# A hybrid decoder trunk: two levels of the gated recurrence per set of small products, with 48 carried query columns

## The chip, the cores and the metric

The kernel runs on one core of a Trainium2 chip. Its time is the device time of one execution in microseconds (us); several executions are taken and their median is compared. A profile is one further execution, recorded by the hardware profiler: its span is the time from the first to the last instruction.

In the text TensorE is PE, its weight loads PEld, VectorE DVE, ScalarE ACT, GpSimd POOL, and SyncE, whose queue issues most DMAs, SP.

## The reference, cut to what matters

Two layers run on 256 tokens of width 1024. Each layer normalises its input, projects it to ten groups of 512 columns, mixes the tokens in three branches (block attention, a gated recurrence named HGRN2, attention to a memory of 256 tokens), gates the result, projects it back and adds it to the input. The change is in the recurrence, which for 4 heads of width 128 computes

```python
qf = jax.nn.silu(q.astype(jnp.float32))
kf = (1.0 - lb) * jax.nn.sigmoid(-fl)
...
diff = A[:, :, :, None, :] - A[:, :, None, :, :]
decay = jnp.exp(jnp.where(causal[:, :, None], diff, -jnp.inf))
scores = jnp.einsum('bhtd,bhtsd,bhsd->bhts', qc, decay, kc)
o = (jnp.einsum('bhts,bhsv->bhtv', scores, vc)
     + jnp.einsum('bhtd,bhdv->bhtv', qc * jnp.exp(A), state))
```

`A` is the running sum of the log of the forget gate. The score of query t with an earlier key s is therefore a sum over 128 channels of q times k times the product of all gates from s+1 to t, a product that differs from channel to channel.

## The kernel before, in words

**The large products.** Weights come from DRAM in 120 chunks of 128x1024 float32 on the SP queue. ACT rounds each chunk to a high part `wh` (L192, or L195 with a gain), DVE subtracts to get the low part `wl` (L204 or L207), and PE multiplies in three products (high by high, high by low, low by high), all recorded at L250. `wr` has four buffers, `wh` and `wl` three each, so a chunk's parts are made while PE works on the one or two chunks ahead of it. The groups of a layer come in the order: memory keys and values, forget gate and query of the recurrence, keys of block attention, input of the recurrence (`ih`), queries of block attention, gate, memory queries, values, two more gates, output projection. A group's results stand in `acc` banks of PSUM, of which there are four; a bank comes free when ACT and DVE have read it.

**The side work.** Everything else is written as Python generators (`g_f`, `g_q`, `g_hgrn`, `g_qk`, ...). The main loop calls `slot()` between pieces of the large products, and each `slot` moves every active generator on to its next `yield`. A scheduler then orders the instructions of each engine; products made through `mm_row` (L254) and some others are kept in program order.

**The recurrence (`g_hgrn`, L773).** Q, K and the gate F lie with channels on partitions and 4 heads x 256 tokens along the free axis. Scores are built by levels. At a level of width m, tokens are taken in pairs of sub-blocks of m; queries of the later one are multiplied by the gates from its start, keys of the earlier one by the gates to its end, and a plain product then gives the scores between the two. `carry` (L783) moves Q and K one level up (DVE, L790 and L791; into a second copy, with ACT copying the unchanged halves, L793 and L794) and multiplies neighbouring gates to the next level's gates T (L797). `diagonal` computes 32 products of 32 keys with 32 query columns each, over 128 channels, for the eight 128-token pieces (4 heads, 2 halves); each lands in one of four 32-partition strips of a PSUM tile `sd`. Two levels go into one tile: a level from `base`, the next from `other`, so 64 products. `keep` (L807) copies those scores to `hSd` that a mask `mk` selects. There are three such blocks of 64 products per layer (levels 0 and 1; 2 and 4; 8 and 16), then a fourth with 16 products of 32 columns and 16 of 64 columns for the widths 32 and 64. The rest of the program calls the blocks the first to the fourth.

**Beside it.** `g_qk` (L902) normalises and rotates q and k of block attention: squares on ACT (L603), sums on DVE (L604), a power on POOL (L915), the rotation on DVE (L918 to L925). The rotary tables `rtA` and `rtB` are made once by `g_setup`: a chain of tiny DVE operations on `rt` (L514 to L542), one Sin on ACT (L543), then POOL (L554 to L558). `g_ih` copies the recurrence's input out of its two banks (ACT, L717).

Of the kernel before, what the change touches and what calls it, by code (L numbers as in the profile page):

```python
# [12 lines left out]
F32 = mybir.dt.float32  # L13
# [32 lines left out]
def hymba_kernel(ctx: ExitStack, tc: tile.TileContext, x, mem, mem_t, positions, w_in, w_out, w_mem_kv,  # L46
# [435 lines left out]
    mk = cst.tile([128, 6, 32], U8, name="mk")  # L482
# [8 lines left out]
    def g_setup():  # L491
# [75 lines left out]
        sp = small("sp", 1)  # L567
        nc.vector.tensor_scalar(sp.bitcast(I32), si, 31, None, op0=OP.bitwise_and)
        ti = sb.tile([128, 32], I32, name="ti", tag="sg", bufs=2)
        nc.gpsimd.iota(ti, pattern=[[1, 32]], base=0, channel_multiplier=0)  # L570
        xi = sb.tile([128, 32], I32, name="xi", tag="sg", bufs=2)
        xf = sb.tile([128, 32], F32, name="xf", tag="sq", bufs=2)
        ge = sb.tile([128, 32], F32, name="ge", tag="sq", bufs=2)
        nc.vector.tensor_tensor(xi, ti, sp.bitcast(I32).to_broadcast([128, 32]), op=OP.bitwise_xor)
        nc.gpsimd.tensor_copy(xf, xi)
        nc.vector.tensor_tensor(xi, ti, sp.bitcast(I32).to_broadcast([128, 32]), op=OP.subtract)
        nc.gpsimd.tensor_copy(ge, xi)
        yield
        nc.gpsimd.tensor_scalar(ge, ge, 0.0, None, op0=OP.is_ge)
        nc.gpsimd.tensor_scalar(xf, xf, 1.0, None, op0=OP.add)  # L580
        nc.gpsimd.tensor_tensor(xf, xf, ge, op=OP.mult)
        for j, m in enumerate((0, 1, 2, 4, 8, 16)):
            nc.gpsimd.tensor_scalar(mk[:, j], xf, float(m + 1), None, op0=OP.is_ge)
# [7 lines left out]
    for tag, n, bufs in (("PTh", 1536, 1), ("PTl", 1536, 1), ("hX", 512, 1), ("qk", 1024, 1), ("sq", 512, 2),  # L591
                         ("vmh", 1024, 1), ("vml", 1024, 1), ("kmh", 1024, 1), ("kml", 1024, 1), ("as", 512, 2),
                         ("al", 256, 2), ("hF", 1024, 1), ("sg", 512, 2), ("ih", 1024, 1),
                         *((f"y{c}{br}", 1024, 1) for br in (H_, A_, M_) for c in "hl"), ("hT1", 512, 1), ("blk", 1536, 1)):
        for _ in range(bufs):
            sb.tile([128, n], F32, name="place", tag=tag, bufs=bufs)
# [105 lines left out]

    def g_q(l, h0, acc):
# [6 lines left out]
        nc.vector.tensor_tensor(T["Q"][:, cs], acc, sg, op=OP.mult)  # L710
# [62 lines left out]
    def g_hgrn(l):  # L773
# [3 lines left out]
        yield from take("PTh", "PTl")  # L777
        Qb = sb.tile([128, 1024], F32, name="hQb", tag="PTh", bufs=1)
        Kb = sb.tile([128, 1024], F32, name="hKb", tag="PTl", bufs=1)
        yield  # L780
# [25 lines left out]
        def keep(g, o, j):  # L806
            nc.vector.copy_predicated(hSd, mk[:, j][:, None, :].to_broadcast([128, 8, 32]),  # L807
                                      g[:, o:o + 256].rearrange("p (a s) -> p a s", s=32))

        nc.vector.tensor_tensor(Qb, Q, F, op=OP.mult)
# [3 lines left out]
        diagonal(g, 0, Q, K)  # L818
        diagonal(g, 256, Qb, K)
        yield 2  # L820
        Tm = carry(1, F, (Qb, K))
        keep(g, 0, 0)
        keep(g, 256, 1)
        rel()
        base, other = (Qb, K), (Q, Kb)
        for m in (2, 8, 32):
            yield
            T2 = carry(m, Tm, base, other)
            yield 2
            yield from room("sd")  # L830
            g = side_tile()
            if m < 32:
                diagonal(g, 0, *base)
                diagonal(g, 256, *other)
            else:
                for a in range(0, 8, 2):
                    for q in (0, 64):
                        for b in range(2):
                            c = (a + b) * 128 + q
                            mm_row(g[q + b * 32:q + b * 32 + 32, a * 16:a * 16 + 32],  # L840
                                   base[1][:, c:c + 32], base[0][:, c + 32:c + 64])
                for a in range(0, 8, 2):
                    for b in range(2):
                        for q in (0, 32):
                            c = (a + b) * 128
                            mm_row(g[b * 64 + q:b * 64 + q + 32, 128 + a * 32:128 + a * 32 + 64],
                                   other[1][:, c + q:c + q + 32], other[0][:, c + 64:c + 128])
            yield 2
            Tm = carry(2 * m, T2, other)
            if m < 32:  # L850
                keep(g, 0, m.bit_length())
                keep(g, 256, m.bit_length() + 1)
                rel()
                base, other = other, base
# [435 lines left out]
```

## Time and profile before

| quantity | value |
|---|---|
| median of 3 runs | 396.36 us (395.73 to 396.39) |
| the profiled execution's own time | 395.6 us |
| its span | 393.8 us |
| PE busy | 388.7 us, 99% of the span |
| DVE busy | 314.8 us, 80% |
| ACT busy | 250.9 us, 64% |
| POOL busy | 70.3 us, 18% |
| granted PE clock | 1.0 |

How to read it: PE is busy nearly all the time, but matmuls are pipelined and their ends are modelled, so a share of busy time does not say how fast PE goes. That is read from the starts of instructions in the timeline and from the waits. A product in full float32 stands in the timeline as two records, so a `diagonal` of 32 products shows as 64. In a timeline row the columns are start, duration, engine, line, operation, output and inputs, shape, count and, in brackets, the idle time before it and what ended it.

### The profile page before, as it was taken

Reading aid. Unit: us, or ns where it says so; the run is one execution under the profiler, and the core shown is the slowest. Engines: PE = TensorE matmul, PEld = TensorE weight load, DVE = VectorE, ACT = ScalarE, POOL = GpSimd, SP = SyncE. Lnnn points to the kernel's source line nnn. Section 1 sums busy time; section 2 is a strip of 40 time slices with the busy share of each in tenths; the row PEclk is TensorE's granted clock in tenths of the full one; section 3 lists DMA queues with packets and bytes.
Section 4 is the critical chain, followed back from the end, with each engine's and each line's share of the span. In section 5 each row is a group of like instructions: output and inputs, shape, how many; then the busy total and the mean of one; then the engine's idle time right before and its main releaser. Section 6 shows DMA issues by size and latency. Waiting matters only on the chain.

```text
span 393.8 us, 7606 instructions
## 1 busy us (share of the span) xinstructions
PE 388.7 (99%) x2871; PEld 325.4 (83%) x2871; DVE 314.8 (80%) x606; ACT 250.9 (64%) x422; POOL 70.3 (18%) x109
## 2 busy tenths in 40 slices
PE   8999999999999999999999999999999999999996
PEld 6888888878788889888888888888888888888885
DVE  4789999889759997964576789799866799897643
ACT  5998746548768759653376665455865894894430
POOL 2013400604202522000000040041150063200000
PEclk9999999999999999999999999999999999999999
DMA  8986674377534989536565658745954189981612
GB/s 280 413 288 222 240 236 156 111 253 227 179 100 169 280 240 327 189 129 207 177 187 173 195 181 229 256 151 158 275 174 155 53 269 272 344 226 67 212 55 107
DMA packets 24900, 80.33 MB, mean 204 GB/s; under 512 B 3232, under 2 KB 5664, under 8 KB 24864
## 3 DMA queue, kind: packets, MB, share of 16 engines
q1 hardware_dynamic: 22304, 71.31, 55.3%
q0 software_dynamic: 2272, 8.39, 7.6%
q8 instruction: 22, 0.36, 0.4%
q10 hardware_dynamic: 288, 0.15, 0.1%
q14 instruction: 14, 0.11, 0.1%
HBM read 72.51 MB, written 7.34 MB: 203 GB/s over the span
## 4 chain that ended last, share of the span: by engine, by line
PE 91%; DVE 4%; POOL 1%; issue 1%; DMA 1%; ACT 1%; ACTq 0%; DVEq 0%
PE acc L250 63%; PE acc L1176 17%; PE sd L250 6%; PE sd L254 4%; DVE wl L204 1%; PE sd L1140 1%; PE sd L463 1%; DMA gT<-in_gains_dram 1%; ACT wh L192 1%; POOL rka L915 1%; PE sd L950 0%; PE sd L1080 0%; POOL rtB L558 0%; DVE hSd L807 0%; DVE hQb L790 0%
## 5 line engine op out<-in xcount | busy, mean ns | idle before, releaser
L204 DVE TENSOR_TENSOR wl<-wr,wh 128x1024 fp32r<-128x1024 f32 x96 | 116.9, 1218 | 40.4 <-ACT wh L192 40.2
L192 ACT CAST wh<-wr 128x1024 fp32r<-128x1024 f32 x96 | 100.8, 1050 | 69.2 <-PE acc L250 42.4
L250 PE MATMUL acc<-wh,hT 128*128 128x512 f32 x384 | 124.8, 396 | 0.0
L250 PEld LDWEIGHTS acc<-wh,hT 128*128 128x128 f32 x384 | 71.8, 188 | 16.1 <-issue 0.7
L250 PE MATMUL acc<-wl,hT 128*128 128x512 f32 x192 | 75.1, 391 | 0.0
L250 PE MATMUL acc<-hT,wh 128*128 128x512 f32 x256 | 65.2, 393 | 0.0
L250 PEld LDWEIGHTS acc<-hT,wh 128*128 128x128 f32 x256 | 45.8, 189 | 8.2 <-ACT kn L617 0.4
L250 PEld LDWEIGHTS acc<-wl,hT 128*128 128x128 f32 x192 | 36.1, 188 | 7.0
L207 DVE SCALAR_TENSOR_TENSOR wl<-wr,gT,wh 128x1024 fp32r<-128x1024 f32 (+1 forms) x29 | 31.2, 1096 | 10.5 <-ACT wh L195 10.3
L195 ACT ACTIVATE wh<-wr,gT 128x1024 fp32r<-128x1024 f32 (+1 forms) x29 | 28.7, 1005 | 14.4 <-PE acc L1176 6.5
L250 PEld LDWEIGHTS acc<-hT,wl 128*128 128x128 f32 x256 | 35.2, 190 | 2.5
L1176 PE MATMUL acc<-wl,yh 128*128 128x512 f32 (+1 forms) x96 | 37.2, 387 | 0.0
L1176 PE MATMUL acc<-wh,yl 128*128 128x512 f32 (+1 forms) x96 | 36.8, 387 | 0.0
L250 PE MATMUL acc<-hT,wl 128*128 128x256 f32 x256 | 36.6, 284 | 0.0
L1176 PE MATMUL acc<-wh,yh 128*128 128x512 f32 (+1 forms) x96 | 30.3, 390 | 0.0
L250 PE MATMUL acc<-wh,mTh 128*128 128x512 f32 x64 | 25.4, 400 | 0.2 <-DVE mTh L402 0.2
L250 PE MATMUL acc<-wh,mTl 128*128 128x512 f32 x64 | 24.8, 390 | 0.0
L1001 ACT ACTIVATE P<-P,nba,rq 128x128 f32<-128x128 f32 (+1 forms) x32 | 17.1, 535 | 8.3 <-DVE nba L995 8.3
L1176 PEld LDWEIGHTS acc<-wh,yh 128*128 128x128 f32 x96 | 18.0, 188 | 3.9 <-issue 0.3
L1176 PEld LDWEIGHTS acc<-wh,yl 128*128 128x128 f32 x96 | 18.0, 188 | 3.7
L1176 PEld LDWEIGHTS acc<-wl,yh 128*128 128x128 f32 x96 | 18.1, 188 | 3.5
L250 PE MATMUL acc<-wl,mTh 128*128 128x512 f32 x64 | 20.2, 392 | 0.0
(222 smaller groups left out, 575.0 us busy)
## 6 DMA issues: line engine op xcount, KB each, us to landing
wr<-in_w_in_dram SPq DMA_DIRECT2D x80, 512.0 KB, 4.3
wr<-in_w_out_dram SPq DMA_DIRECT2D x24, 512.0 KB, 4.4
wr<-in_w_mem_kv_dram SPq DMA_DIRECT2D x15, 512.0 KB, 4.4
there<-blk POOLq DMA_DIRECT2D x4, 768.0 KB, 5.4
PT<-there POOLq DMA_DIRECT2D x16, 192.0 KB, 6.0
there<-blk SPq DMA_DIRECT2D x4, 512.0 KB, 3.7
xs<-in_x_dram SPq DMA_DIRECT2D x2, 512.0 KB, 8.6
memr<-in_mem_dram SPq DMA_DIRECT2D x2, 512.0 KB, 6.7
```

The source lines that it names most:

```text
L192: nc.scalar.copy(whs[i], raws[i])
L195: nc.scalar.activation(whs[i][:, sl], raws[i][:, sl], AF.Copy, scale=gT[:, g:g + 1])
L204: nc.vector.tensor_tensor(wls[i], raws[i], whs[i].bitcast(F32), op=OP.subtract)
L207: ins = nc.vector.scalar_tensor_tensor(wls[i][:, sl], in0=raws[i][:, sl], scalar=gT[:, g:g + 1], in1=whs[i][:, sl].bitcast(F32), op0=OP.mu ...
L250: nc.tensor.matmul(o, lhsT=a, rhs=b, start=s, stop=e)
L254: tc.keep_in_program_order(nc.tensor.matmul(o, lhsT=a, rhs=b, start=s, stop=e))
L463: ins = nc.tensor.transpose(pt[:, j * 256 + t * 128:j * 256 + (t + 1) * 128], xn[t][:, k * 128:(k + 1) * 128], ident)
L915: nc.gpsimd.tensor_tensor(r[:, t8], ms[:, t8], pw[:, :8], op=OP.pow)
L1001: nc.scalar.activation(P[:, i, kc[t]], P[:, i, kc[t]], AF.Exp, bias=nb[:, c:c + 1], scale=rq[:, r:r + 1], accum_out=sm[:, c:c + 1])
L1140: nc.tensor.transpose(pt[:, i * 256 + t * 128:i * 256 + (t + 1) * 128], P[:, t, i, b * 128:(b + 1) * 128], ident)
L1176: ins = nc.tensor.matmul(a, lhsT=y, rhs=wt[:, cs], start=n == (0 if to is None else nk - 2) and j == 0, stop=n == nk - 1 and j == 2)
```

## The change

The three blocks of 64 products of 32 columns become three blocks of 32 products of 48 columns. Keys are no longer carried for the second level of a block: both levels of a block use the same 32 key columns, and the queries are laid out several times instead. In the first block each pair of tokens has three query columns: both queries as they are, and the later one carried over one token. In the second (m = 2) and the third (m = 8), each four sub-blocks of m tokens have six sub-blocks of query columns: the second, third and fourth as they stand at their own start, the third and fourth carried back over one more sub-block, the fourth carried over two. The fill and the carries of the queries move to new operations; `g_q` writes Q twice with a stride of three (now in the buffer PTh); there are eight masks in place of six and eight `keep` operations in place of six, on fewer columns each. The fourth block and all behind it stay as they were.

The core of the diff, without the set-up of the masks:

```diff
-            T["Q"] = sb.tile([128, 1024], F32, name="hQ", tag="hq0", bufs=1)
+            yield from take("PTh", "PTl")
+            T["Q"] = sb.tile([128, 512, 3], F32, name="hQ1", tag="PTh", bufs=1)
...
-        nc.vector.tensor_tensor(T["Q"][:, cs], acc, sg, op=OP.mult)
+        nc.vector.tensor_tensor(T["Q"][:, h0 * 128:h0 * 128 + 256, 0:2], pairs(acc, 2), pairs(sg, 2), op=OP.mult)
...
-        def diagonal(g, o, q, k):
+        def row(q, m):
+            g = side_tile()
             for i in range(8):
                 for j in range(4):
-                    c = slice(i * 128 + j * 32, i * 128 + j * 32 + 32)
-                    mm_row(g[j * 32:j * 32 + 32, o + i * 32:o + i * 32 + 32], k[:, c], q[:, c])
+                    c = i * 4 + j
+                    mm_row(g[j * 32:j * 32 + 32, i * 48:i * 48 + 48].rearrange("p (n m) -> p n m", m=m),
+                           K[:, c * 32:c * 32 + 32], q(c))
...
-        nc.vector.tensor_tensor(Qb, Q, F, op=OP.mult)
+        nc.vector.tensor_tensor(Q[:, :, 2], Q[:, :, 1], F2[:, :, 1], op=OP.mult)
         yield 2
         yield from room("sd")
-        g = side_tile()
-        diagonal(g, 0, Q, K)
-        diagonal(g, 256, Qb, K)
+        g = row(lambda c: Q[:, c * 16:c * 16 + 16], 3)
+        Tm = sb.tile([128, 512], F32, name="hT1", tag="hT1", bufs=1)
+        nc.vector.tensor_tensor(Tm, F2[:, :, 0], F2[:, :, 1], op=OP.mult)
         yield 2
-        Tm = carry(1, F, (Qb, K))
-        keep(g, 0, 0)
-        keep(g, 256, 1)
-        rel()
-        base, other = (Qb, K), (Q, Kb)
-        for m in (2, 8, 32):
...
+        n4 = sb.tile([128, 128, 7, 2], F32, name="hQ2", tag="PTl", bufs=1)
+        nc.vector.tensor_tensor(n4[:, :, 0:4], Q[:, :, 0:3:2].rearrange("p (g a) i -> p g a i", a=4),
+                                F2[:, :, 0].rearrange("p (g a) -> p g a", a=4)[:, :, :, None]
+                                .to_broadcast([128, 128, 4, 2]), op=OP.mult)
+        nc.vector.tensor_tensor(K2[:, :, 0], K2[:, :, 0], F2[:, :, 1], op=OP.mult)
+        keep(g[:, :, :, 0:2], 0, 2, 0, 2)
+        keep(g[:, :, :, 2:3], 1, 2, 1, 2)
+        rel()
+        for m in (2, 8):
...
+            nc.vector.tensor_tensor(q[:, :, 4:6], q[:, :, 2:4], by(1, 2), op=OP.mult)
+            nc.vector.tensor_tensor(q[:, :, 6:7], q[:, :, 5:6], by(1, 1), op=OP.mult)
+            yield 2
+            yield from room("sd")
+            b = 8 // m
+            g = row(lambda c: q[:, c * b:c * b + b, 1:7].rearrange("p g a i -> p g (a i)") if b > 1
+                    else q[:, c, 1:7].rearrange("p a i -> p (a i)")[:, None, :], 6 * m)
+            nc.vector.tensor_tensor(T4[:, :, 2], T4[:, :, 2], T4[:, :, 3], op=OP.mult)
+            nc.vector.tensor_tensor(T4[:, :, 1], T4[:, :, 1], T4[:, :, 2], op=OP.mult)
+            Tn = sb.tile([128, n], F32, name=f"hT{m}", tag=f"hT{m}", bufs=1)
+            nc.vector.tensor_tensor(Tn, T4[:, :, 0], T4[:, :, 1], op=OP.mult)
+            yield 2
...
+            nc.scalar.copy(to(0, 1), split(q[:, :, 0:1]))
+            nc.vector.tensor_tensor(to(1, 1), split(q[:, :, 1:2]), split(by(0, 1)), op=OP.mult)
+            nc.vector.tensor_tensor(to(2, 2), split(q[:, :, 4:7:2]), split(by(0, 1, 2)), op=OP.mult)
+            nc.vector.tensor_tensor(K4[:, :, 0:3], K4[:, :, 0:3], by(1, 3), op=OP.mult)
+            for k, (lo, hi, at) in enumerate(((1, 4, 0), (2, 4, 3), (3, 4, 5))):
+                keep(g[:, :, :, at * m:(at + hi - lo) * m], (2 if m == 2 else 5) + k, 4 * m, lo * m, hi * m)
+            rel()
+            Tm = Tn
+        base = n4, K
+        other = [sb.tile([128, 1024], F32, name=n, tag=t, bufs=1) for n, t in (("hQb", "PTl"), ("hKb", "PTh"))]
```

The scheduler also orders the neighbourhood anew; lines below the change carry higher numbers in the changed kernel. Three places of layer 0 matter to what follows.

PE around the third block, before. The names `acc_1164` and `acc_1165` are the two banks (tokens 0 to 127 and 128 to 255) of the group that follows, the queries of block attention:

```order
L250 MATMUL acc_927<-wh_903,hT_160 128x512
L254 MATMUL sd_1096<-hQ_712,hKb_792 32x32 x32
L254 MATMUL sd_1096<-hQb_791,hK_591 32x32 x32
L250 MATMUL acc_1164<-wh_949,hT_160 128x512
L250 MATMUL acc_1164<-wl_1044,hT_160 128x512
L250 MATMUL acc_1164<-wh_949,hT_160 128x512
L250 MATMUL acc_1165<-wh_949,hT_160 128x512
```

and in the changed kernel, where the same two banks are named `acc_1070` and `acc_1071`:

```order
L254 MATMUL sd_1018<-hQ3_982,hK_592 32x48 x32
L250 MATMUL acc_1070<-wh_913,hT_160 128x512
L250 MATMUL acc_1070<-wl_980,hT_160 128x512
L250 MATMUL acc_1070<-wh_913,hT_160 128x512 x2
L250 MATMUL acc_1070<-wl_980,hT_160 128x512
L250 MATMUL acc_1070<-wh_913,hT_160 128x512
L250 MATMUL acc_1070<-wh_978,hT_160 128x512
L250 MATMUL acc_1070<-wl_1009,hT_160 128x512
L250 MATMUL acc_1070<-wh_978,hT_160 128x512 x2
L250 MATMUL acc_1070<-wl_1009,hT_160 128x512
L250 MATMUL acc_1070<-wh_978,hT_160 128x512
L250 MATMUL acc_1070<-wh_1007,hT_160 128x512
```

The two products by 32 columns became one by 48, and the group behind them now does twelve products of its first bank before it touches its second. Its banks are other ones than before: in the placement of the built program they were those of the block-attention keys, and are now those that `ih` is copied out of.

ACT around the Sin of the rotary tables (`sc_164`), before:

```order
L603 ACTIVATE sq<-acc 128x512
L543 ACT_TABLE_LOAD
L543 ACTIVATE sc_164<-rt 128x32
L192 CAST wh<-wr 128x1024
L793 COPY hQb<-hQ 128x64x8
L192 CAST wh<-wr 128x1024
L794 COPY hK<-hKb 128x64x8
L192 CAST wh<-wr 128x1024
L717 COPY ih<-acc 128x512
L192 CAST wh<-wr 128x1024
L717 COPY ih<-acc 128x512
```

and in the changed kernel:

```order
L599 ACTIVATE sq<-acc 128x512
L863 COPY hQ<-hQ_982 128x32x8
L192 CAST wh<-wr 128x1024 x2
L789 COPY hQb<-hQ 128x16x32
L192 CAST wh<-wr 128x1024
L543 ACT_TABLE_LOAD
L543 ACTIVATE sc_164<-rt 128x32
L717 COPY ih<-acc 128x512
L192 CAST wh<-wr 128x1024
L717 COPY ih<-acc 128x512
L790 COPY hKb<-hK 128x16x32
```

The Sin moved behind three casts and the copy of the fourth block's queries, and stands directly ahead of the first copy of `ih`.

DVE ahead of the `wl` of the first chunk of that group (chunk 24 of 120), before; `tm` is a piece of the rotation of the keys, and waits for `rtB`:

```order
L790 TENSOR_TENSOR hQ<-hQ,hT_938 128x128x4
L920 TENSOR_TENSOR tm<-acc,rtB 128x8x8
L922 TENSOR_TENSOR tm<-acc,rtB 128x8x8
L920 TENSOR_TENSOR tm<-acc,rtB 128x8x8
L922 TENSOR_TENSOR tm<-acc,rtB 128x8x8
L791 TENSOR_TENSOR hKb<-hKb,hT_938 128x128x4
L807 COPY_PREDICATED hSd<-mk,sd 128x256
L790 TENSOR_TENSOR hQb<-hQ,hT_1054 128x64x8
L925 TENSOR_TENSOR kr<-kr,tm 128x8x16 x2
L791 TENSOR_TENSOR hK<-hKb,hT_1054 128x64x8
L807 COPY_PREDICATED hSd<-mk,sd 128x256
L204 TENSOR_TENSOR wl<-wr,wh 128x1024
```

and in the changed kernel, from the `wl` of chunk 23 to that of chunk 24:

```order
L204 TENSOR_TENSOR wl<-wr,wh 128x1024
L951 TENSOR_SCALAR msa<-ssa 128x8
L866 TENSOR_TENSOR hK<-hK,hT_844 128x128x6
L808 COPY_PREDICATED hSd<-mk,sd 128x32x6
L865 TENSOR_TENSOR hQ<-hQ_982,hT_952 128x32x16
L843 TENSOR_TENSOR hT_952<-hT_952 128x32
L541 TENSOR_SCALAR rt<-rt 128x16
L204 TENSOR_TENSOR wl<-wr,wh 128x1024
```

The rotation of the keys no longer stands between the two `wl`; it moved behind the `wl` of chunk 26.

More of the change, by code (lines that the diff above doesn't have):

```diff
@@ L565, in g_setup @@
         nc.gpsimd.memset(hSd, 0.0)
[L567 to L577, printed above, removed]
-        yield
[L579 to L583, printed above, removed]
+        d = sb.tile([128, 3, 32], I32, name="ti", tag="sg", bufs=2)
+        for q, w in enumerate((1, 2, 8)):
+            nc.gpsimd.iota(d[:, q], pattern=[[1, 32 // w], [0, w]], base=0, channel_multiplier=0)
+        sp = small("sp", 3)
+        xf = sb.tile([128, 3, 32], F32, name="xf", tag="sq", bufs=2)
+        for q, w in enumerate((0, 1, 3)):
+            j = sp[:, q:q + 1].bitcast(I32)
+            nc.vector.tensor_scalar(j, si, 31, w, op0=OP.bitwise_and, op1=OP.logical_shift_right)
+            nc.vector.tensor_tensor(d[:, q], d[:, q], j.to_broadcast([128, 32]), op=OP.subtract)
+        nc.gpsimd.tensor_copy(xf, d)
+        yield
+        for j, (q, least) in enumerate(((0, 0), (0, 1), (1, 1), (1, 2), (1, 3), (2, 1), (2, 2), (2, 3))):
+            nc.gpsimd.tensor_scalar(mk[:, j], xf[:, q], float(least), None, op0=OP.is_ge)
     setup = g_setup()
@@ L776, in g_hgrn @@
         St = hST.rearrange("p h t s -> p (h t) s")
[L777 to L780, printed above, removed]
         def halves(a, m):
@@ L814, in g_hgrn, with keep, part @@
-        nc.vector.tensor_tensor(Qb, Q, F, op=OP.mult)
+                    c = i * 4 + j
+                    mm_row(g[j * 32:j * 32 + 32, i * 48:i * 48 + 48].rearrange("p (n m) -> p n m", m=m),
+                           K[:, c * 32:c * 32 + 32], q(c))
+            return g[:, :384].rearrange("p (a n m) -> p a n m", a=8, m=m)
+        def keep(g, j, n, lo, hi):
+            def part(a):
+                return a.rearrange("p a (n m) -> p a n m", m=n)[:, :, :, lo:hi]
+            nc.vector.copy_predicated(part(hSd), part(mk[:, j][:, None, :].to_broadcast([128, 8, 32])), g)
@@ L815, in g_hgrn @@
+        base = n4, K
+        other = [sb.tile([128, 1024], F32, name=n, tag=t, bufs=1) for n, t in (("hQb", "PTl"), ("hKb", "PTh"))]
+        yield
+        T2 = carry(32, Tm, base, other)
         yield 2
@@ L817, in g_hgrn @@
         g = side_tile()
-        diagonal(g, 0, Q, K)
-        diagonal(g, 256, Qb, K)
-        yield 2
-        Tm = carry(1, F, (Qb, K))
-        keep(g, 0, 0)
-        keep(g, 256, 1)
-        rel()
-        base, other = (Qb, K), (Q, Kb)
-        for m in (2, 8, 32):
[L827 to L830, printed above, removed]
-            g = side_tile()
[L832 to L854, printed above, removed]
+        for a in range(0, 8, 2):
+            for q in (0, 64):
+                for b in range(2):
+                    c = (a + b) * 128 + q
+                    mm_row(g[q + b * 32:q + b * 32 + 32, a * 16:a * 16 + 32],
+                           base[1][:, c:c + 32], base[0][:, c + 32:c + 64])
+        for a in range(0, 8, 2):
+            for b in range(2):
+                for q in (0, 32):
+                    c = (a + b) * 128
+                    mm_row(g[b * 64 + q:b * 64 + q + 32, 128 + a * 32:128 + a * 32 + 64],
+                           other[1][:, c + q:c + q + 32], other[0][:, c + 64:c + 128])
+        yield 2
+        carry(64, T2, other)
         S2 = St.rearrange("p (a b) s -> p a b s", b=2)
```

31 lines of the change are left out of this document (26 added, 5 removed).

## The prediction

> **What bounds the kernel now.** I read the page, then who PE waits for, then the chain of work that ended last. From the page, the span and the busy time of each engine:
>
> ```profile
> span 393.8 us, 7606 instructions
> ## 1 busy us (share of the span) xinstructions
> PE 388.7 (99%) x2871; PEld 325.4 (83%) x2871; DVE 314.8 (80%) x606; ACT 250.9 (64%) x422; POOL 70.3 (18%) x109
> ```
>
> All waits of PE, longest first (us in total, times, longest):
>
> ```profile
> PE sd L250 <- DVE dm L378: 1.0, 1, 1.0
> PE sd L254 <- ACT wh L192: 0.2, 1, 0.2
> PE acc L250 <- DVE mTh L402: 0.2, 1, 0.2
> ```
>
> PE waits 1.4 us in all, 1.2 of it at the start. The kernel is bound by PE's own work: a product left out shortens it by what that product takes on PE, unless a new wait eats the gain. The chain (start, us, what) runs over PE in layer 1 and shows the four blocks, L254, among large products. Its counts mix loads and records, so only its times are used:
>
> ```profile
> 85.59 0.65 PE sd L254 x32
> ...
> 106.02 1.96 PE sd L254 x24
> ...
> 252.42 1.23 PE sd L254 x82
> ...
> 260.69 1.30 PE sd L254 x98
> ...
> 269.01 1.30 PE sd L254 x98
> ...
> 277.33 0.88 PE sd L254 x63
> ```
>
> The three blocks of 1.23, 1.30 and 1.30 us are what the change cuts; layer 0 has the same three. In layer 0 the chain comes onto PE only at 85.59, in the fourth block. (106.02 is the first use of the attention keys `kT`.)
>
> **PE, the main term.** The timeline of PE in layer 1 (start, us, and at the end the count of records), second and fourth block:
>
> ```profile
> 260.62 0.76 PE L254 MATMUL sd<-hQb,hK 128*32 128x32 f32 x64
> 261.23 0.75 PE L254 MATMUL sd<-hQ,hKb 128*32 128x32 f32 x64
> 261.92 0.50 PE L250 MATMUL acc<-wh,hT 128*128 128x512 f32 x1
> ...
> 277.26 0.46 PE L254 MATMUL sd<-hQb,hK 128*32 128x32 f32 x32
> 277.54 0.68 PE L254 MATMUL sd<-hQ,hKb 128*32 128x64 f32 x32
> 278.14 0.50 PE L250 MATMUL acc<-wh,hT 128*128 128x512 f32 x1
> ```
>
> Starts are what counts. From 260.62 to 261.23, 64 records of 32 columns take 0.61 us, 9.5 ns each; the next 64 take 0.69 to the first large product, so 0.08 is the change back. With 64 columns, 32 records take 0.60 - 0.08 = 0.52 us, 16.3 ns each. The trace has no record of 48 columns. It lies between these two, and I take the middle, 12.9 ns, since the price already grows with the columns. A block then has 64 records of 12.9 ns and the change, 0.83 + 0.08 = 0.91 us, against 1.23, 1.30 and 1.30: 3.83 - 2.73 = 1.1 us a layer, 2.2 us for both. At the price of 32 columns a block takes 0.69 and both layers give 3.5 us; at the price of 64 it takes 1.12 and they give 0.9. The number of changes between small and large products stays as it is.
>
> Here the Trainium skill has a rule: "TensorEngine Tiling (Array Packing)", section Instruction Overhead, says that each matmul has about 60 cycles of overhead, so that fewer columns than that cost the same. By it 48 columns cost what 32 do, and the two layers would give 3.5 us. The rows show a price that grows from 32 to 64, 9.5 to 16.3 ns, which speaks against it; it is a rival below.
>
> **The waits in layer 0.** PE's timeline at the first large products behind the third block, and in the fourth block:
>
> ```profile
> 77.84 0.50 PE L250 MATMUL acc<-wh,hT 128*128 128x512 f32 x1
> 78.18 0.48 PE L250 MATMUL acc<-wl,hT 128*128 128x512 f32 x1
> ...
> 84.95 0.46 PE L254 MATMUL sd<-hQb,hK 128*32 128x32 f32 x32
> 85.59 0.65 PE L254 MATMUL sd<-hQ,hKb 128*32 128x64 f32 x32 [0.17 <-ACT wh L192]
> ```
>
> and DVE's around them:
>
> ```profile
> 61.16 1.22 DVE L204 TENSOR_TENSOR wl<-wr,wh 128x1024 fp32r<-128x1024 f32 x1 [0.27 <-ACT wh L192]
> 62.30 0.26 DVE L521 SCALAR_TENSOR_TENSOR rt<-rt 128x16 f32<-128x16 f32 x2
> ...
> 73.48 0.23 DVE L920 TENSOR_TENSOR tm<-acc,rtB 128x64 f32<-128x64 f32 x1 [1.75 <-POOL rtB L557]
> ...
> 76.90 1.20 DVE L204 TENSOR_TENSOR wl<-wr,wh 128x1024 fp32r<-128x1024 f32 x1
> ...
> 84.76 0.68 DVE L791 TENSOR_TENSOR hKb<-hK,hT 128x512 f32<-128x512 f32 x1
> ```
>
> The 32 records that took 0.28 us in layer 1 (277.26 to 277.54) take 0.64 here, so 0.36 us are a wait. The profile names ACT's cast, but the 64-column products read DVE's carried keys, and L791 ends at 85.44, just ahead. And the `wl` of chunk 24 ends at 78.10 and is read at 78.18: DVE is 0.08 us ahead. DVE's order here decides whether the gain stays.
>
> **DVE and ACT.** Durations by form, from the groups of instructions (us in all, mean ns of one):
>
> ```profile
> L755 DVE TENSOR_TENSOR ys<-sd,zT 128x512 f32<-128x512 f32 x8 | 5.4, 680 | 0.0
> ...
> L807 DVE COPY_PREDICATED hSd<-mk,sd 128x256 f32<-128x256 uint8 x12 | 5.3, 443 | 0.0
> ...
> L814 DVE TENSOR_TENSOR hQb<-hQ,hF 128x1024 f32<-128x1024 f32 x2 | 2.5, 1226 | 0.0
> ...
> L790 DVE TENSOR_TENSOR hQb<-hQb,hF 128x512 f32<-128x512 f32 x2 | 1.4, 684 | 0.0
> ...
> L797 DVE TENSOR_TENSOR hT<-hT 128x256 f32<-128x256 f32 x2 | 0.8, 420 | 0.0
> ```
>
> This L790 reads and writes every second element and takes 684 ns, the plain L755 680, so I price strided and broadcast forms by their elements alone, 1.06 ns each beyond 512 ((1226 - 684) / 512): 768 elements 0.95 us, 128 some 0.28. Before, DVE does 14 carries of 0.68, L814 with 1.23, and 2.0 for the gates T: 12.8 us a layer. Now it does eleven operations of 512 (Q's third column, T, K, two more at each of two levels, four for the widths 32 and 64), 7.5; the tile of 1024, 1.23; four of 256, 1.7; two of 768, 1.9; smaller ones for T, 1.6: 13.9 us, 1.1 more. The eight `keep` cover 1152 columns where six covered 1536, about 2.6 us either way by 443. ACT loses four copies a layer and gains two of half the size. In layer 1 all this lies beside the large products. Layer 0 is walked through by the changed order, each operation starting its duration less 0.08 behind the last, as 62.30 follows 61.16. ACT's rows for it:
>
> ```profile
> 66.39 1.28 ACT L543 ACT_TABLE_LOAD   x1
> 67.68 0.23 ACT L543 ACTIVATE sc<-rt 128x32 f32<-128x32 f32 x1
> ...
> 76.27 0.57 ACT L717 COPY ih<-acc 128x512 f32<-128x512 f32 x1
> ```
>
> The queries of levels 2 and 4 are made ahead of the `wl` of chunk 21, which slips from 61.16 to about 61.4 and takes 1.1. From there to the end of L865 at the second level stand two `wl`, six operations of 512, three of 256, two of 128, one of 768, three `keep` and small ones, 10.0 us: L865 ends near 72.6, and the `wl` of chunk 24 near 73.9. PE reads it at 78.18 less the 1.1 it has gained, 77.1: DVE is 3.2 us ahead instead of 0.08, because the rotation of the keys has left this path. Behind it come the fourth block's queries, two `wl`, then `tm`, which waits for POOL. The Sin starts near 75.5 (below) and not at 67.68. POOL's steps from there to the first `rtB` took until 73.48, 5.8 us, with 2.1 of L915 between that now go first: `tm` starts near 79.2, the keys' carry ends near 81.9, and the fourth block, wanted at 84.95 - 1.1 = 83.9, waits no more: 0.36 us gained. The `wl` of chunk 27 ends near 84.5, two us ahead of its use. The keys' transpose then sends `kT` 4 to 5 us later on SP, past one more load; its first use at 106.02 leaves that covered. The masks come from POOL long before their use.
>
> **The sum.** 2.2 + 0.36 = 2.6 us. The profiled execution, 395.6 us with 1.8 outside its span, would come to 393.0. It lies 0.8 under the median of the runs, so from 396.36 I forecast 393.8 us.
>
> **The rivals.** *48 columns at the price of 32.* 3.5 + 0.36 leave 392.5 us. For it: the four strips work at once, and what else bounds 9.5 ns is not shown. Against it: the growth to 16.3. The page's rule of 60 cycles says the same.
>
> *Part of the gain is lost.* 48 columns at the price of 64 give 0.9 + 0.36, 395.1 us; a new wait of 1.3 us on PE gives the same.
>
> *PE waits for the banks of `ih`, and it is slower.* The queries of block attention now use the banks that L717 empties, behind the Sin. Behind L865 at 72.6 follow the copy L789 (0.6), a cast (1.0), the table load (1.3), the Sin and the first L717 (0.7): the bank is free near 76.2. PE wants it at 77.84 - 1.1 = 76.7, so 0.5 us are left. Each further us on this path stalls PE by one; from 3.1 nothing is gained, from 3.9 it is slower. The new strided forms ahead of L865 hold 5376 elements; if they cost twice as much, 5.7 us, PE waits 5.2 and the time is 399.0 us. Against: 684 beside 680. The Trainium skill, "ScalarE: Activation LUTs", section What ACT_TABLE_LOAD costs, adds a drain of about 1.38 us to every table load; an estimate from it is a wait of 0.9 here, 394.7 us. The trace disagrees: the Sin starts 1.29 us after its load began.
>
> *Nothing comes of it.* At half more for the strided forms PE waits 2.3 us, and 396.1 us is no difference.
>
> **How the numbers follow.** Chances: forecast 0.54, price of 32 columns 0.14, part lost 0.19, nothing 0.08, slower 0.05. About 0.2%, 0.8 us, is what a measurement can tell here, so under 395.6 is faster. The first two cases and three quarters of the third are: 0.82. Within 0.2% is the rest of the third and the fourth, 0.13; slower 0.05. The price of 48 columns alone runs from 392.5 to 395.1; the range, 392.4 to 395.7, takes this in, and leaves out the last two cases and a little of the third.
>
> **What would show it.** Right: L254 has 64 records a block, starting near 12.9 ns apart; blocks near 0.9 us in the chain; the `wl` of chunk 24 some 3 us ahead of its use; no wait of PE at the fourth block of layer 0 nor behind the third. Wrong: the first large product behind the third block starts late with ACT's L717 as what it waited for; L835 or L865 takes well over 0.7 us; blocks still take 1.2.

## The result and the profile after

| quantity | before | after |
|---|---|---|
| median of 6 runs | 395.85 us (395.73 to 396.39) | 392.64 us (392.32 to 393.37) |
| the profiled execution's own time | 395.6 us | 392.6 us |
| its span | 393.8 us | 390.8 us |

The ratio is 0.9918, 95% interval 0.9908 to 0.9928: 3.2 us less. The forecast was 2.6 us less, 393.8 us, and 0.5 of the 1.16 us between it and 392.64 is that it started from a median of three runs, 396.36, where six gave 395.85. The other 0.6 is gain that the forecast did not have.

The page of the changed kernel, span and busy times:

```profile
span 390.8 us, 6833 instructions
## 1 busy us (share of the span) xinstructions
PE 385.8 (99%) x2487; PEld 322.9 (83%) x2487; DVE 316.2 (81%) x621; ACT 248.0 (63%) x418; POOL 73.4 (19%) x109
```

All its waits of PE (us in total, times, longest):

```profile
PE sd L250 <- DVE dm L378: 1.0, 1, 1.0
PE acc L250 <- ACT mTh L404: 0.3, 1, 0.3
```

Both are at the start. The wait in layer 0's fourth block is gone and none has taken its place. The chain that ended last, the blocks of small products (start, us):

```profile
60.59 0.82 PE sd L254 x64
67.75 0.82 PE sd L254 x64
75.82 0.82 PE sd L254 x64
84.11 0.88 PE sd L254 x63
...
251.20 0.82 PE sd L254 x64
```

Blocks of 1.23, 1.30 and 1.30 us have become 0.82 each, in both layers: 1.37 us a layer. The chain now runs over PE in layer 0 too. PE's timeline in the fourth block of layer 0:

```profile
84.04 0.46 PE L254 MATMUL sd<-hQ,hK 128*32 128x32 f32 x32
84.31 0.68 PE L254 MATMUL sd<-hQb,hKb 128*32 128x64 f32 x32
```

From start to start the 32 records take 0.27 us here, 0.64 before.

**A ruler that the start does not bend.** PE's first us differ by up to 2.7 us between the traces: its waits for the first chunks differ, and in two traces (rot24 and late1) the granted clock is 0.5 for 3.4 us near the start. So the kernels below are also compared by the starts of large products (outputs named `acc`), of which every trace has 1568: from the 61st to the last; from the 241st to the 601st, which holds layer 0's blocks; from the 1001st to the 1301st, which holds layer 1's. Stretches without blocks agree: before and after, from the 601st to the 1001st both take 92.45 us.

| kernel | median, us | 61st to last | layer 0 | layer 1 |
|---|---|---|---|---|
| before | 395.85 | 369.79 | 95.37 | 82.51 |
| after | 392.64 | 366.64 | 93.55 | 81.18 |
| cols64 | 394.15 | 367.84 | 94.18 | 81.73 |
| cols32 | 392.9 | 366.64 | 93.55 | 81.17 |
| two24 | 396.95 | 370.45 | 95.74 | 82.80 |
| rot24 | 396.82 | 370.25 | 95.92 | 82.41 |
| strips | 402.28 | 376.20 | 98.36 | 85.94 |
| parts | 425.39 | 400.32 | 110.12 | 98.25 |
| later3 | 395.95 | 369.43 | 95.05 | 82.52 |
| late1 | 394.54 | 368.08 | 94.98 | 81.18 |
| layer1 | 395.72 | 369.31 | 96.36 | 81.08 |
| dve2 | 393.12 | 366.66 | 93.54 | 81.21 |
| mg12 | 392.98 | 366.43 | 93.16 | 81.33 |
| mgx | 392.68 | 365.91 | 93.16 | 80.81 |

Experiments ran on chips on which the kernel before took 396.15 to 396.46 us, so their medians stand 0.3 to 0.6 us high beside the first two rows. parts was executed four times, and two of them ran at a lower granted clock and longer (430.87 and 432.31 us), so its row has the median of the two others.

By the ruler the change gains 3.15 us: 1.82 in layer 0 and 1.33 in layer 1. Layer 0 has the same 1.37 of the blocks and the 0.36 of the wait; under 0.1 us is left over. The scheduler orders every kernel anew: later3 has PE's order of before, but for the block that was moved, and late1 that of the changed kernel until after the fourth block; in most of the others some block stands a few large products elsewhere, and it is said where that matters.

### The profile page after: what moved, and what is told of

It is laid out like the page before. It is cut to its first block, busy times and chain, and to the rows that moved or that the text cites. A ratio compares the mean times of both kernels' runs of the same rounds, so it can differ in the third digit from the quotient of the medians.

```text
span 390.8 us, 6833 instructions
## 1 busy us (share of the span) xinstructions
PE 385.8 (99%) x2487; PEld 322.9 (83%) x2487; DVE 316.2 (81%) x621; ACT 248.0 (63%) x418; POOL 73.4 (19%) x109
## 4 chain that ended last, share of the span: by engine, by line
PE 98%; DMA 1%; DVE 0%; ACT 0%; issue 0%; DVEq 0%
PE acc L250 69%; PE acc L1213 17%; PE sd L250 6%; PE sd L254 4%; PE sd L1177 1%; PE sd L463 1%; DMA gT<-in_gains_dram 1%; PE sd L987 0%; PE sd L1117 0%; ACT wh L195 0%; DVE xs L1247 0%; DVE xs L1254 0%; ACT mTh L404 0%; DVEq L1254 0%
## 5 line engine op out<-in xcount | busy, mean ns | idle before, releaser
L250 PE MATMUL acc<-wh,hT 128*128 128x512 f32 x384 | 122.9, 394 | 0.0
L195 ACT ACTIVATE wh<-wr,gT 128x1024 fp32r<-128x1024 f32 (+1 forms) x29 | 28.7, 1006 | 14.3 <-PE acc L1213 6.5
L1038 ACT ACTIVATE P<-P,nba,rq 128x128 f32<-128x128 f32 (+1 forms) x32 | 17.1, 536 | 8.3 <-DVE nba L1032 8.3
L952 POOL TENSOR_TENSOR rka<-msa,pw 128x8 f32<-128x8 f32 x4 | 9.9, 2475 | 58.2 <-DVE msa L951 58.2
```

The lines of the kernel that those rows point to most:

```text
L195: nc.scalar.activation(whs[i][:, sl], raws[i][:, sl], AF.Copy, scale=gT[:, g:g + 1])
L250: nc.tensor.matmul(o, lhsT=a, rhs=b, start=s, stop=e)
L952: nc.gpsimd.tensor_tensor(r[:, t8], ms[:, t8], pw[:, :8], op=OP.pow)
L1038: nc.scalar.activation(P[:, i, kc[t]], P[:, i, kc[t]], AF.Exp, bias=nb[:, c:c + 1], scale=rq[:, r:r + 1], accum_out=sm[:, c:c + 1])
```

## The experiments

Theory A is that of the prediction, in the sizes that the trace of the changed kernel shows: PE bounds, a small product's price grows with its columns, and DVE's order in layer 0 decides whether the gain stays.

### What a product of 48 columns costs: cols64 and cols32

```diff
-                    mm_row(g[j * 32:j * 32 + 32, i * 48:i * 48 + 48].rearrange("p (n m) -> p n m", m=m),
-                           K[:, c * 32:c * 32 + 32], q(c))
+                    w = 64 if c < 31 else s
+                    mm_row(g[j * 32:j * 32 + 32, i * 64:i * 64 + w], K[:, c * 32:c * 32 + 32],
+                           q[:, c * s:c * s + w])
```

> The changed kernel with its 48 query columns widened to 64 (31 of 32 products of a block; the 16 more are computed and not used). Theory A, a record's price grows with its columns: in the changed kernel's trace four records of 48 columns, one for each strip, take 42.5 ns and four of 64 columns in the fourth block 55.8, 10.6 and 14.0 ns a record. A block grows by 62 x 3.4 ns = 0.21 us, from 0.82 to 1.03; six blocks give 1.3 us, 393.9 us. Theory B, a product has a price of its own and columns do not count up to 64: blocks stay at 0.82 and the time at 392.6 us.

The first block in the chain, and the others are like it:

```profile
60.97 1.02 PE sd L254 x62
```

0.20 more a block; six are 1.2, and the ruler has 367.84 - 366.64 = 1.20. Theory A holds.

```diff
-                    mm_row(g[j * 32:j * 32 + 32, i * 48:i * 48 + 48].rearrange("p (n m) -> p n m", m=m),
+                    mm_row(g[j * 32:j * 32 + 32, i * 32:i * 32 + 32], K[:, c * 32:c * 32 + 32], q(c))
```

> The changed kernel with 32 of the 48 query columns in every product of the three blocks; a third of the scores is left out, DVE's work stays as it is. Theory A, the price grows with the columns: 8.0 ns a record as in the fourth block, 64 x 2.6 ns = 0.17 us less a block, 1.0 us in all, 391.6 us. Theory B, a price a product whatever its columns: 392.6 us, no change.

In the chain the first block of layer 1 and what the fourth became; then two of PE's waits:

```profile
251.33 0.69 PE sd L254 x50
...
273.19 0.39 PE sd L254 x32
276.52 0.58 PE sd L254 x32
```

```profile
PE acc L250 <- ACT ih L717: 0.3, 1, 0.3
PE acc L250 <- ACT wh L195: 0.2, 1, 0.2
```

The blocks came out near theory A, 0.13 less each where it had 0.17, and yet nothing is gained. In layer 0 the 0.39 us of three blocks meet a wait of 0.3 us that the changed kernel does not have, for the copy L717: the bank of `ih`. (The wait for L195 is at the start.) In layer 1 the scheduler split the fourth block in two (0.39 and 0.58 beside 0.88), and one more change between small and large products took the gain. The first is the prediction's third rival, at work here with PE less than 0.4 us earlier.

### Whether few columns stay cheap: two24, parts, rot24, strips

Each product as two of 24 columns, one behind the other in the same strip:

```diff
-                    mm_row(g[j * 32:j * 32 + 32, i * 48:i * 48 + 48].rearrange("p (n m) -> p n m", m=m),
-                           K[:, c * 32:c * 32 + 32], q(c))
+                    for u in range(2):
+                        o = i * 48 + u * 24
+                        mm_row(g[j * 32:j * 32 + 32, o:o + 24].rearrange("p (n m) -> p n m", m=min(m, 24)),
+                               K[:, c * 32:c * 32 + 32], q(c, u))
```

> The changed kernel with every product of 48 columns made as two of 24, twice the records and the same columns. Theory A, a straight line through 8.0 ns at 32 and 10.6 at 48 columns: 24 columns 6.7 ns, 128 records 0.86 us against 0.68, 0.18 more a block, 1.1 us in all, 393.7 us. Theory B, a record does not get cheaper than the 8.0 ns that 32 columns take: 128 x 8.0 = 1.02 us, 0.34 more a block, 2.1 us in all, 394.7 us. Theory C, columns alone count: no change, 392.6 us.

The first block of layer 1 in the chain, like the other two there:

```profile
254.42 1.38 PE sd L254 x102
```

1.38 us a block, over all three expectations. The kernel parts does the same in three pieces of 16 columns and four of 12.

```diff
-                    mm_row(g[j * 32:j * 32 + 32, i * 48:i * 48 + 48].rearrange("p (n m) -> p n m", m=m),
-                           K[:, c * 32:c * 32 + 32], q(c))
+                    z = 48 // parts
+                    for u in range(parts):
+                        o = i * 48 + u * z
+                        mm_row(g[j * 32:j * 32 + 32, o:o + z], K[:, c * 32:c * 32 + 32], q(c, u))
```

> The changed kernel with each product of the first and third block made as three of 16 columns, and of the second as four of 12. Theory A, the straight line: 5.4 ns a record at 16 columns, 4.8 at 12; the blocks take 192 x 5.4 + 0.14 = 1.18, 256 x 4.8 + 0.14 = 1.37 and 1.18 us against 0.82, 1.3 us more a layer, 2.5 in all, 395.2 us. Theory B, a floor at the 8.0 ns of 32 columns: 1.68, 2.19 and 1.68 us, 3.1 us more a layer, 6.2 in all, 398.8 us. Theory C, columns alone count: no change, 392.6 us.

All theories missed by far: 425.39 us. By the single starts of its records four products of 16 columns take about 120 ns and four of 12 about 153, where four of 48 took 85. Its waits of PE show a second cost, time in which PE waits for nothing that this view shows:

```profile
PE sd L254 <- issue: 5.2, 5, 2.0
PE acc L250 <- issue: 2.0, 1, 2.0
```

The granted PE clock on its page shows a third; each digit is a fortieth of the span:

```profile
PEclk9999998989999999999999999979899999999999
```

In the trace the clock is 0.5 in four stretches, 17.1 us together, and each begins 0.1 to 1.3 us behind one of the four longest of these waits; a large product starts every 0.43 us there instead of every 0.23. Of the 33.7 us that parts has more on the ruler, the waits are 7.2, the halved clock some 8 (an estimate: 17.1 us at 0.23 / 0.43 of the pace) and the records themselves the rest. The page also has what the waits may be for. One of the queues carries instructions (packets, MB, share of the DMA engines):

```profile
q8 instruction: 26, 0.43, 0.4%
```

That is 26 packets of 16 KB, where the kernel before has 22, and each of the six waits ends 1.2 to 1.6 us after one of them has landed. It looks as if PE waited for its own instructions; that is read from the times, and no run tests it.

All three theories had left out the order. In these two kernels products of one strip follow each other; in the changed kernel the four strips take turns. No run has pieces of 16 or 12 columns with the strips in turn, so how much of their price is the order stays open. For two pieces of 24 and for whole products it was tested. So rot24 is two24 with its loops exchanged,

```diff
-                for j in range(4):
-                    c = i * 4 + j
-                    for u in range(2):
+                for u in range(2):
+                    for j in range(4):
+                        c = i * 4 + j
                         o = i * 48 + u * 24
```

> The same two products of 24 columns for each of 48 as in the run before it, but in another order: four products to the four 32-partition strips in turn, then the second four, where the run before made both products of a strip one behind the other and took 1.38 us a block. Theory S, a product holds its strip until it is done and only products of other strips run beside it: one product of 24 columns took 38 ns there (two a strip in 1.24 us over 32 pairs), four in turn then share 38 to 45 ns; 64 products take 0.61 to 0.72 us, the block 0.75 to 0.86, the time 392.2 to 392.9 us. Theory P, products of few columns are dear by themselves: the block stays near 1.38 and the time near 397 us.

and strips is the changed kernel strip by strip.

```diff
-            for i in range(8):
-                for j in range(4):
+            for j in range(4):
+                for i in range(8):
```

> The changed kernel with its products of 48 columns in another order: the eight of one strip, then the eight of the next, instead of the four strips in turn. Theory S: a product of 48 columns alone takes the 85 ns in which four now start, 32 of them 2.7 us, a block 2.9 instead of 0.82; six blocks add 12 us, 405 us. Theory P, the order does not count: 392.6 us.

One block in the chain of rot24, then one in that of strips; the others are the same:

```profile
255.93 1.21 PE sd L254 x82
```

```profile
60.99 2.42 PE sd L254 x64
```

The order counts: strip by strip the same products take 2.42 instead of 0.82 us, (2.42 - 0.14) / 32 = 71 ns a product beside 21; six blocks are 9.6 us and the ruler has 9.56. The 71 is a mean, and it is less than the 85 of theory S because of the changes from strip to strip. Inside a strip a record starts 42 or 43 ns behind the last, so a product alone takes the 85 ns expected; at each of the three changes seven starts follow each other in 158 ns instead of 298, which saves 0.42 us a block. So a record of 48 columns keeps its strip for 42.5 ns, and the four strips work side by side: with the strips in turn four records start in the same 42.5. In rot24 neither theory is right: turns make the block 0.17 shorter, but 1.21 is not 0.86. A record of 24 columns takes 8.3 ns there (eight starts in 66 to 67), as much as one of 32. So there is a floor. In long stretches of two24, too, four records take 33 ns; its 0.17 us more lie in irregular stretches between. The median of rot24 hardly differs from two24's, because a wait of 0.7 us by the starts, for DVE's `tm`, stands in its layer 0; layer 1, without waits, has 82.41 beside 82.80.

The price of a record with the strips in turn, from the single starts, is then 8.3 ns at 24 columns, 8.0 at 32, 10.6 at 48 and 14.0 at 64. The last two are 0.22 ns a column, and by that 32 columns would be 7.0: about 8 is the least that a record took in any of these runs. What sets this floor, they don't show.

Here two pages of the Trainium skill can be held against rows. "TensorEngine Tiling (Array Packing)", section Instruction Overhead, says that products under some 60 columns cost the same: the trace agrees for 24 and 32 columns, not for 48. "TensorE: Matmul & The Clock Gate", section Wait — 56ns, not 53.3ns?, gives N / 2.4 GHz plus about 2.5 ns from start to start, and never under about 25 ns. If a record is two passes of its columns through one strip, an estimate from that page is 42.5 ns at 48 columns and 55.8 at 64 for four records, one in each strip; the trace has 42.5 and 55.8, and strips has 42.5 for one record in one strip. For 24 columns it gives 25, and the trace has 33. The two passes are an assumption that no run tests.

### The waits of layer 0: later3 and late1

The fourth block of the kernel before, moved behind six more large products:

```diff
-            yield 2
+            yield 3 if l == 0 and m == 32 else 2
```

> The kernel before, with the fourth block of layer 0 six large products later, and nothing else of PE's order moved before it. If the 0.36 us that its 32 records took too long is a wait for the carried keys that ends at the same time in any case, it vanishes: the 32 records take 0.28 us, the span is 393.4 and the time 0.36 us less, 395.5 us beside 395.85. If the kernel is late there for another reason, PE waits as long in the new place.

Its timeline there:

```profile
87.01 0.46 PE L254 MATMUL sd<-hQb,hK 128*32 128x32 f32 x32
87.28 0.68 PE L254 MATMUL sd<-hQ,hKb 128*32 128x64 f32 x32
```

The 32 records take 0.27 us, as in the changed kernel, and the ruler has 0.36 less, layer 0 alone 0.32. The wait was one, of the predicted size, and the other layer does not change (82.52). The ratio of the runs, 0.9987 (0.9977 to 0.9998), points the same way, but is too coarse to size it.

Now the other wait, which the prediction feared. In late1 the last L865 of layer 0 is made twice:

```diff
-            nc.vector.tensor_tensor(to(2, 2), split(q[:, :, 4:7:2]), split(by(0, 1, 2)), op=OP.mult)
+            for _ in range(2 if l == 0 and m == 8 else 1):
+                nc.vector.tensor_tensor(to(2, 2), split(q[:, :, 4:7:2]), split(by(0, 1, 2)), op=OP.mult)
```

> The changed kernel, in layer 0 with the last L865 made twice, 0.6 us more of DVE's time ahead of the copy L789, the table load, the Sin and the first L717. In the order of this kernel the bank then comes free 1.0 us later than the 76.51 of the changed kernel. The trace of the changed kernel has the bank free 0.06 us ahead of PE; PE then waits 0.9 us there, naming L717, and the time is 393.5 us. By the 0.5 us of slack that the prediction worked out the wait is 0.5 and the time 393.1. If the wait is made good by a later one, no change.

The changed kernel's ACT there, its PE, and late1's PE (the last bracket is the idle time and who ended it):

```profile
74.50 1.28 ACT L543 ACT_TABLE_LOAD   x1
75.79 0.23 ACT L543 ACTIVATE sc<-rt 128x32 f32<-128x32 f32 x1
75.92 0.57 ACT L717 COPY ih<-acc 128x512 f32<-128x512 f32 x1
```

```profile
76.56 0.50 PE L250 MATMUL acc<-wh,hT 128*128 128x512 f32 x1
```

```profile
80.53 0.50 PE L250 MATMUL acc<-wh,hT 128*128 128x512 f32 x1 [1.33 <-ACT ih L717]
```

L717 ends at 76.49 in the changed kernel and PE takes the bank at 76.56: 0.07 us to spare. In late1 PE waits 1.33 us for that copy, and the ruler has 1.44 more, all in layer 0 (94.98 - 93.55); layer 1 is the same to 0.01. So what is late here costs one to one and no later wait makes it good. 0.6 us of DVE's work cost more than twice itself: a `wl` was put between the two L865, and ACT, which waits for the second one in L789, came later by that too. I had expected 0.9. In late1 the carries L865 stand in line 866, and the second one and the copy are

```profile
77.05 0.69 DVE L866 TENSOR_TENSOR hQ<-hQ,hT 128x512 f32<-128x512 f32 x1
```

```profile
77.83 0.62 ACT L789 COPY hQb<-hQ 128x512 f32<-128x512 f32 x1 [1.08 <-DVE hQ L866]
78.48 1.28 ACT L543 ACT_TABLE_LOAD   x1
```

All of late1 runs 2.56 us later there (its third block starts at 78.31 and not at 75.75). Less that, L789 comes 2.37 us later than the 72.90 of the changed kernel, and the table load 1.42, because the cast that stood between the two now goes ahead of L789. Of the 1.42 the slack takes 0.07: that is the wait.

### One layer alone, and DVE's cover: layer1 and dve2

In layer1 `g_q` and `g_hgrn` of the kernel before run for layer 0, with their six masks, and the new ones for layer 1:

```diff
     def g_q(l, h0, acc):
+        if l == 0:
+            yield from g_q0(l, h0, acc)
+            return
```

> The change in layer 1 alone; layer 0 as before, with the masks of both. If PE's own time is all that counts, the three blocks of layer 1 take 0.82 us each instead of 1.23, 1.30 and 1.30, 1.37 us less, and the time is 394.5 us beside 395.85; by the price of the prediction 1.1 us less, 394.75. If DVE's and ACT's extra work in layer 1 costs something, or the gain of 3.2 us is mostly the waits of layer 0, less than 1 us is gained.

Layer 1 gains 82.51 - 81.08 = 1.43 us, as expected. Layer 0, whose code is that of before, loses 0.99, so that the median is 395.72 where the kernel before had 396.15 on that chip, and not the 1.37 less that was expected. PE and DVE show why:

```profile
79.69 0.50 PE L250 MATMUL acc<-wl,hT 128*128 128x512 f32 x1 [1.20 <-DVE wl L204]
```

```profile
77.23 1.27 DVE L1140 TENSOR_TENSOR kr<-kr,rka 128x512 f32<-128x512 f32 x2
78.43 2.35 DVE L204 TENSOR_TENSOR wl<-wr,wh 128x1024 fp32r<-128x1024 f32 x2
```

The tiny operations for a second set of masks changed the scheduler's order: the last step of the rotation of the keys (here L1140) now stands ahead of the `wl` of chunk 24, which in the kernel before was 0.08 us ahead of PE. PE's start on it comes 1.70 us behind the large product before, where it was 0.34: 1.36 us late, and a wait is there that no line of the edit speaks of. The wait of the fourth block, 0.36, is gone in return. So the 0.08 was as thin as it looked; the 3 us of cover that the changed kernel has there instead are seen below.

In dve2 the four L835 and L865 of layer 1 are made twice:

```diff
-            nc.vector.tensor_tensor(q[:, :, 4:6], q[:, :, 2:4], by(1, 2), op=OP.mult)
+            for _ in range(2 if l else 1):
+                nc.vector.tensor_tensor(q[:, :, 4:6], q[:, :, 2:4], by(1, 2), op=OP.mult)
```

> The changed kernel with four DVE operations of 512 elements in layer 1 made twice (L835 and L865 at both levels), 2.7 us more of DVE's work. If DVE's work in layer 1 lies beside the large products, as the prediction says, nothing changes: 392.6 us and no wait of PE there. If DVE sets the pace of the blocks, up to 2.7 us more, 395.3.

Layer 1 takes 81.21 beside 81.18, and PE waits for nothing there, as the prediction said. But the scheduler made room for it: the third and fourth block of layer 1 stand 24 and 23 large products later than in the changed kernel. So the run shows that 2.7 us more of DVE's work can lie beside the large products, not that the old order would have held it.

### A version from it: mg12 and mgx

The traces show a fixed part of every block, the change between small and large products: 0.33 us. Blocks one behind the other save one.

```diff
+            if m == 2 or not m34:
+                g = third()
+            if m == 2 and m12:
+                g1 = first()
...
+        if m34:
+            far()
+            near()
+            g3 = third()
```

`first` and `third` are the calls of `row` for the first and for the second or third block, held back; `far` and `near` are the halves of the fourth block. The block that is ready last goes first, so that the scheduler puts nothing between. `m12` and `m34` say in which layers.

> The changed kernel with small blocks put one behind the other: first and second together in both layers, third and fourth together in layer 1; keys carried for the later block go to buffers of their own, for which ACT copies the unchanged parts (five copies more in all, 0.4 to 0.6 us each). Theory F, each change between large and small products costs PE the same whatever the block holds: in the changed kernel 0.318 us pass from the last large start to the first small one, 0.136 from the last small to the first large and 0.336 to the next, against 0.227, 0.011 and 0.227 without a change, 0.33 us in all. Three changes fewer give 1.0 us, 391.6 us. Theory W, the merged blocks reach a wait (the third block of layer 0 covers the copies of ih): PE waits as long as it gains, 392.6 us.

In the chain, the first and second block of layer 0, and the third and fourth of layer 1:

```profile
66.18 1.50 PE sd L254 x128
...
278.54 1.59 PE sd L254 x124
```

A pair takes 1.50 where two blocks took 1.64, and one way in and out, 0.09 and 0.11, goes with it: theory F's price. Layer 0 gains 0.39. Layer 1, with both pairs, loses 0.15: PE waits for two `wl`, and with the longer step behind each wait they cost 0.29 and 0.55 us. Theory W was right there, with `wl` for the banks. I put this down to the carries of keys and queries, which all come behind the first pair. DVE's row just ahead of the first of these `wl` (265.49) names another cause:

```profile
264.28 0.69 DVE L1019 TENSOR_TENSOR kr<-kr,rka 128x512 f32<-128x512 f32 x1 [1.17 <-POOL rka L997]
```

The new order put a step of the rotation of the keys there, for which DVE stood idle 1.17 us, waiting for POOL; in the changed kernel that step stands behind this `wl` and the next one. mgx, made on my first reading, keeps one pair a layer, the first in layer 0 and the second in layer 1.

> The changed kernel with the first and second block together in layer 0 alone, and the third and fourth in layer 1 alone. In the run with three merged pairs, PE's stretch with the blocks of layer 0 became 0.39 us shorter, and that of layer 1, with both pairs, 0.15 longer: two wl there came 0.29 and 0.55 us late, behind DVE's carries that all wait for the first merged block. Theory F with that cause: both stretches now shrink by 0.33 us, PE waits for no wl, and the time is 0.7 us less than the changed kernel's 392.64, 392.0 us. If the later wl in layer 1 come late by the merged third and fourth blocks, layer 1 gains nothing: 392.3 us.

```profile
65.93 1.50 PE sd L254 x128
...
251.18 0.82 PE sd L254 x64
...
275.05 1.59 PE sd L254 x124
```

The three rows are the pair in layer 0, a single block and the pair in layer 1. In mgx that step of the rotation stands behind both `wl` again. PE waits at the start alone, and the ruler has 365.91, 0.73 us less than the changed kernel, 0.39 and 0.37 by layer. It is the shortest of all by the ruler. Against the kernel before, its ratio is 0.9911, 0.9891 to 0.9931, and that of the changed kernel 0.9918: runs of this number do not separate the two.

## Why the prediction was right, and where it was off

**PE bounds, one to one.** Right. cols64 and strips moved the ruler by what their blocks took longer, to 0.05 us, and layer1 by what the blocks of layer 1 took less, to 0.06.

**The price of 48 columns.** This is the term that was mis-sized, and it carries nearly all of the error in the gain. I took the middle of the prices of 32 and 64 columns, 12.9 ns a record and 0.91 us a block; it is 10.6, and 0.82: 1.37 us a layer instead of 1.1, 2.7 instead of 2.2. Two things were wrong in the step. Both ends were too high, because I divided whole stretches by their number of records: 9.5 and 16.3 ns, while the even part has 8.0 and 14.0. In those stretches some starts lie further apart, 33 ns behind the fourth record and 45 at the change of level. That is 1.9 of the 2.3 ns. And the middle of two prices is right only on a straight line: 32 columns lie on the floor, 48 above it, and at 48 and 64 the price is proportional. Against this the way back to the large products, 0.08 in my sum, takes 0.14. The rule of the Trainium skill ("TensorEngine Tiling (Array Packing)", section Instruction Overhead), which I made a rival, has a floor, as the trace has, and puts it too high: by it both layers would give 3.5 us, where 2.7 came.

**The wait of the fourth block.** Right: 0.36 us, by later3 and by 0.27 us for the 32 records in the changed kernel.

**The walk through layer 0.** DVE's rows of the changed kernel:

```profile
72.15 0.66 DVE L865 TENSOR_TENSOR hQ<-hQ,hT 128x512 f32<-128x512 f32 x1
...
72.94 1.21 DVE L204 TENSOR_TENSOR wl<-wr,wh 128x1024 fp32r<-128x1024 f32 x1
...
79.76 0.22 DVE L957 TENSOR_TENSOR tm<-acc,rtB 128x64 f32<-128x64 f32 x1 [0.46 <-POOL rtB L557]
...
81.83 0.68 DVE L787 TENSOR_TENSOR hKb<-hK,hT 128x512 f32<-128x512 f32 x1
```

L865 ends at 72.8 (forecast 72.6), the `wl` of chunk 24 at 74.2 (73.9), `tm` starts at 79.8 (79.2), the keys' carry ends at 82.5 (81.9), ahead of the fourth block at 84.0. The `wl` of chunk 24 is 2.8 us ahead of its use, forecast 3.2.

**The rival with the banks of `ih`.** It did not strike, but the step under it was off: the bank comes free at 76.49 and not 76.2, PE takes it at 76.56 and not 76.7, and 0.07 us are left of my 0.5. late1 and cols32 show that the mechanism is real and that each us late is a us lost. A tenth of a us more on that path would have begun to eat the gain: that it did not strike was near to luck.

**Strided forms by their elements.** Right for most, wrong for one kind. In the groups of the changed kernel (us in all, mean ns of one):

```profile
L866 DVE TENSOR_TENSOR hK<-hK,hT 128x768 f32<-128x768 f32 x4 | 3.8, 951 | 0.0
...
L865 DVE TENSOR_TENSOR hQ<-hQ,hT 128x512 f32<-128x512 f32 x4 | 2.7, 681 | 0.0
...
L812 DVE TENSOR_TENSOR hQ<-hQ,hF 128x512 f32<-128x512 f32 x2 | 1.7, 870 | 0.0
...
L842 DVE TENSOR_TENSOR hT<-hT 128x128 f32<-128x128 f32 x2 | 0.8, 408 | 0.0
```

951 for 768 elements and 681 for 512 are what I reckoned. L812, at a stride of three elements, takes 870 instead of 684, and L842, at four, 408 instead of 280. The Trainium skill, "SBUF — State Buffer", section Specifications (TRN2), has lines of 16 bytes that need two hits each for full bandwidth. The trace agrees: a stride of two float32 has two hits and 684 ns, three and four have fewer and cost more. No run varies the stride alone.

**DVE in all.** 314.8 became 316.2 us, 1.4 more where I had 2.2, beside the large products.

## What to carry to other kernels

Small products that share PE in strips are cheap only while the strips take turns; count their price as the greater of a floor and a rate by columns, both read from single starts of records, and not as a middle of two averages. On a kernel whose PE never waits, a saving is worth its full time only as far as the next buffer's slack reaches: here 0.07 us, and in layer 0 a third of the columns less gave nothing. Where a scheduler sets the order, an edit elsewhere can move a `wl` past its slack, so slacks under 0.1 us are to be read before and after.

## What the runs showed of the hardware

- Products of 48 columns took 21 ns each with the four strips in turn. Inside one strip they took 85, and 71 in the mean of a block that goes strip by strip (strips). Two of 24 columns, one behind the other in a strip, cost 1.38 us a block, and 1.21 with the strips in turn.
- A float32 record of 24 columns cost as much as one of 32 (8.3 and 8.0 ns, strips in turn); at 48 and 64 columns it cost 0.22 ns a column. By these the floor would end near 36 columns, an estimate: nothing between 32 and 48 was run.
- A change between small and large products and back cost PE 0.32 to 0.34 us for blocks of 32, 48 and 64 columns.
- parts, with 896 records more than the changed kernel, had six waits, 7.2 us in all, in which PE waited for nothing that the profile names, each ending 1.2 to 1.6 us after a 16 KB packet of instructions had landed. Behind the four longest the granted clock was 0.5, for 17.1 us together. With 384 records more (two24, rot24) no such wait came.
